# Mixing weights of a dilated-attention kernel: statistics loaded by GpSimd's queue, small operations moved to GpSimd and spread over steps, additions later, chunks closer

## The chip, the core and the metric

The kernel runs on one core of a Trainium2 chip. The metric is the device time of one execution in microseconds (us); the median of several runs counts.

## What is computed

One layer of a decoder trunk over 2048 tokens and 1024 channels, in float32. Half of the channels go through eight attention heads of 64, the other half through pooling groups; both are projected by `w_out`; then come a gated MLP and a gated per-layer embedding. The change is in the attention. Each head attends in three patterns, and the outputs are mixed by their softmax denominators:

```python
DIL_PATTERNS = ((128, 1), (512, 4), (2048, 16))
...
for window, dil in DIL_PATTERNS:
    o, m, d = _dilated_branch(q, k, v, slopes, window, dil)   # output, row max, denominator
...
w = d * jnp.exp(m - jnp.max(m, axis=0, keepdims=True))
w = w / jnp.sum(w, axis=0, keepdims=True)
return jnp.sum(w[..., None] * o, axis=0)
```

## The kernel before

It runs in three phases: projection, attention, and the rest (output projection, MLP, gate). Matrix products are made from split operands: a rounded high part and the remainder as a low part. The attention phase lies at about 389 to 655 us.

**The steps of the attention.** The kernel merges the two wider patterns into one, called far; the narrow one is near. So each query has two outputs, near and far, and two pairs of statistics (`st1` near, `st3` far: row extremum, with the sign turned so that it is a minimum, and denominator). The work is cut into 128 steps s: 8 heads by 16 blocks of 128 queries. A pair of heads takes 32 steps. One step holds far and near scores on TensorE (L568 to L580), a reduction for each on VectorE (L584 near, L590 far), an exponential for each on ScalarE (L596, L600), transposes on TensorE (L610), the high part on ScalarE (L623) and the low part on VectorE (L627), and the products with the values on TensorE (L638 far, L652 near). Stages of one query block stand in different steps; the list `CFG["ord"]` gives each stage's place in a step and its lag. On TensorE, VectorE, ScalarE and GpSimd the program's order is kept as written. The order of the transfers that SyncE issues is made by the scheduling layer.

**Copying out.** Every four steps a group of queries is done. `copy_out` (L670 on) copies the output from PSUM to a buffer `ev` (far by ScalarE, near by VectorE, L676), has SyncE move one half of it across partitions into `s1` or `s3` (L677), and puts an addition of the other half on GpSimd (L678) three steps later.

**Mixing.** When the first, second and third pair of heads has ended, its two outputs are mixed while the next pair runs. d counts the steps from the pair's end (`mix`, L727 on):

- at the end `mix_stats` (L788) transposes the statistics on TensorE and copies them to SBUF on VectorE; at d = 1 ScalarE's queue stores them to DRAM (L803, L804);
- at d = 4 ScalarE's queue loads them back in another layout (L811 `sn`, L815 `sf`), each load 512 pieces of 64 bytes;
- at d = 9 `mix_lift` (L885): on VectorE the minimum `lo` (L889) and two differences `ex` (L892, L893), on ScalarE the exponential `wts` (L894);
- at d = 10 `mix_weights` (L897): on VectorE two products and a sum, the denominator `dn` (L901 to L903), its reciprocal `rs` (L905) and the weights (L906); GpSimd's queue stores them (L907);
- for each of four chunks c of 512 queries, `mix_fetch` (L912) at d = 13 + 7c has SyncE load the weights broadcast over partitions, and `mix_steps` (L940) six steps later begins two products and a sum on GpSimd (L946, L948, L955) and a store of the mixed chunk (L958). After the third pair, which is called quick, the fetches are at d = 12 + 4c, and two parts are issued a step.

The fourth pair is mixed at the end of the phase by other code. `last_weights` (L847) makes its weights on VectorE and ScalarE, and its scratch `lo` shares the buffers `m1` with the chunks.

Of the kernel before, what the change touches and what calls it, by code (L numbers as in the profile page):

```python
# [10 lines left out]
F32 = mybir.dt.float32  # L11
F32R = mybir.dt.float32r
AF = mybir.ActivationFunctionType
ALU = mybir.AluOpType
# [3 lines left out]
P = 128  # L18
# [8 lines left out]
CH = 512  # L27
# [16 lines left out]
CFG = {"tt": 2, "ee": 2, 'ord': [['B', 0], ['G', 0], ['M', 0], ['h', 2], ['N', 0], ['F', 0], ['nm', 0], ['p', 7], ['o', 8], ['ne', 0], ['V', 6], ['fm', 0], ['l', 2], ['W', 6], ['S', 1], ['fe', 0], ['T', 1]], 'perm': [3, 1, 2, 0], 'fp': [[0], [1], [2], [3]], 'np': [[0, -1], [1], [2], [3]], 'm': [9, 10, 13, 4, 6, 7]}  # L44
# [6 lines left out]
def fp(ap):  # L51
    return ap.bitcast(F32)
# [439 lines left out]
def phase_attention(tc, g, mx, near_b, far_b):  # L492
# [3 lines left out]
    nc = tc.nc  # L496
    NS = H * NQ
    LAST = 4 * H - 2
    with ExitStack() as ctx:
        sb = ctx.enter_context(tc.tile_pool(name="b_sb", bufs=1, reuse_waits="tile"))  # L500
# [5 lines left out]
        heads, steps, groups, pairs = {}, {}, {}, {}  # L506
# [155 lines left out]
        sums = Ticker()  # L662

        def halves(pt, gi, near):
            h, q = divmod(gi, 4)
            e = h % 2
            mine = slice(DH * e, DH * e + DH)
            other = slice(DH * (1 - e), DH * (1 - e) + DH)
            return e, mine, other, pt.s1[:, q * CH : (q + 1) * CH] if near else pt.s3[:, q, :]

        def copy_out(copy, gi, near):

            e, mine, other, dst = halves(pairs[gi // 8], gi, near)
            o = groups[gi].o[near]
            t = sb.tile([P, CH], F32, tag="ev", bufs=8, name="ev")
            copy(t, o)  # L676
            nc.sync.dma_start(dst[mine], t[other])  # L677
            sums.later(3, lambda: nc.gpsimd.tensor_tensor(dst[mine], dst[mine], t[mine], op=ALU.add))  # L678

        def add_out(gi, near):  # L680
            e, mine, other, dst = halves(pairs[gi // 8], gi, near)
# [25 lines left out]
        def fold(v):  # L707
            gi, part = v // 4, v % 4
            if part == 1 and gi < LAST:
                copy_out(nc.scalar.copy, gi, False)  # L710

        def folded(v):
            gi, part = v // 4, v % 4
            if part % 2 and gi >= LAST:
                add_out(gi, part == 3)
            elif part == 3:
                copy_out(nc.vector.tensor_copy, gi, True)
            if part == 3:
                groups.pop(gi)
# [7 lines left out]
        def mix(s):  # L727
            for pr in range(NPAIR - 1):
                d = s - (pr + 1) * 2 * NQ
                if d == 1:  # L730
                    mix_stats_store(nc, g, pr, pairs[pr])
                if d == 4:
                    mix_stats_load(nc, g, mx, pr, pairs[pr])
                if d == CFG["m"][0]:
                    mix_lift(nc, g, mx, pairs[pr])
                if d == CFG["m"][1]:
                    mix_weights(nc, g, mx, pr, pairs[pr])
                for c in range(NCH):
                    quick = pr == NPAIR - 2
                    at = d - (12 + 4 * c if quick else 13 + 7 * c)  # L740
                    if at == 0:
                        mix_fetch(nc, g, mx, nc.sync, pr, pairs[pr], c)
                    if at == 6:
                        ops[pr, c] = mix_steps(nc, g, mx, pr, pairs[pr], c)
                    for _ in range(1 + quick if (pr, c) in ops else 0):
                        next(ops[pr, c], None)
# [6 lines left out]
        with tc.manual_schedule(engines=set(EN.values())):  # L753
            for dst, src in load_qk(0):
                rdma(nc, dst, src)
            for q in range(4):
# [3 lines left out]
            stages = {  # L760
                "F": far_scores, "N": near_scores, "fm": far_max, "nm": near_max, "fe": far_exp, "ne": near_exp,
                "T": turn, "h": high, "l": low, "V": values, "W": values_b, "S": stats, "M": mix, "o": fold, "p": folded, "B": begin, "G": shifts
            }
            for s in range(NS + 10):
# [37 lines left out]
def mix_stats_store(nc, g, pr, pt):  # L802
    nc.scalar.dma_start(g.std[pr], pt.sx)  # L803
    nc.scalar.dma_start(g.stf[pr], pt.sy)  # L804


def mix_stats_load(nc, g, sb, pr, pt):
    q = nc.scalar
    pt.sn = sb.tile([P, 2, 2, 16], F32, tag="sn", name="sn")
    pt.sf = sb.tile([P, 2, 2, 16], F32, tag="sf", name="sf")  # L810
    q.dma_start(  # L811
        pt.sn.rearrange("p a e r -> p (a e) r"),
        g.std[pr].rearrange("(ae n) q -> ae (n q)", n=NQ).rearrange("ae (i r) -> i ae r", r=16),
    )
    q.dma_start(  # L815
        pt.sf.rearrange("p a e r -> p (a e) r"),
        g.stf[pr].rearrange("(ae n) q -> ae (n q)", n=4).rearrange("ae (i r) -> i ae r", r=16),
    )
# [28 lines left out]
def last_weights(nc, sb, pt):  # L847

    both = (pt.near, pt.far)
    lo = sb.tile([P, CH], F32, tag="m1", bufs=2, name="lo")[:8]  # L850
    nc.vector.tensor_tensor(lo, pt.near[0], pt.far[0], op=ALU.min)
    yield
    for mx_, _ in both:
        nc.vector.tensor_tensor(mx_, lo, mx_, op=ALU.subtract)
    yield
    for ex, _ in both:
        nc.scalar.activation(ex, ex, AF.Exp)
    yield
    for ex, dn in both:
        nc.vector.tensor_tensor(dn, ex, dn, op=ALU.mult)  # L860
    yield
    nc.vector.tensor_tensor(lo, pt.near[1], pt.far[1], op=ALU.add)
    yield
    nc.vector.reciprocal(lo, lo)
    yield
    pt.w = []
    for ex, _ in both:
        hi, low = (sb.tile([P, CH], F32R, tag=f"wb{y}", bufs=2, name=f"w{y}")[:8] for y in range(2))
        nc.vector.tensor_tensor(ex, ex, lo, op=ALU.mult)
        nc.scalar.copy(hi, ex)  # L870
        nc.vector.tensor_tensor(low, ex, fp(hi), op=ALU.subtract)
        pt.w.append((hi, low))
    yield
# [11 lines left out]
def mix_lift(nc, g, sb, pt):  # L885

    sn, st3 = pt.sn, pt.sf
    lo = sb.tile([P, 2, 16], F32, tag="lo", name="lo")
    nc.vector.tensor_tensor(lo, sn[:, 0], st3[:, 0], op=ALU.min)  # L889
    pt.wts = sb.tile([P, 2, 2, 16], F32, tag="wts", name="wts")  # L890
    ex = sb.tile([P, 2, 2, 16], F32, tag="ex", name="ex")
    nc.vector.tensor_tensor(ex[:, 0], lo, sn[:, 0], op=ALU.subtract)  # L892
    nc.vector.tensor_tensor(ex[:, 1], lo, st3[:, 0], op=ALU.subtract)  # L893
    nc.scalar.activation(pt.wts, ex, AF.Exp)  # L894


def mix_weights(nc, g, sb, pr, pt):  # L897

    sn, st3, wts = pt.sn, pt.sf, pt.wts
    dn = sb.tile([P, 2, 2, 16], F32, tag="dn", name="dn")  # L900
    nc.vector.tensor_tensor(dn[:, 0], wts[:, 0], sn[:, 1], op=ALU.mult)  # L901
    nc.vector.tensor_tensor(dn[:, 1], wts[:, 1], st3[:, 1], op=ALU.mult)
    nc.vector.tensor_tensor(dn[:, 0], dn[:, 0], dn[:, 1], op=ALU.add)  # L903
    rs = sb.tile([P, 2, 16], F32, tag="rs", name="rs")
    nc.vector.reciprocal(rs, dn[:, 0])  # L905
    nc.vector.tensor_tensor(wts, wts, rs[:, None, :, :].to_broadcast([P, 2, 2, 16]), op=ALU.mult)  # L906
    nc.gpsimd.dma_start(  # L907
        g.wd[pr].rearrange("ae (i r) -> i ae r", r=16), wts.rearrange("p a e r -> p (a e) r")
    )


def mix_fetch(nc, g, sb, q, pr, pt, c, bufs=2):  # L912

    cs = slice(c * CH, (c + 1) * CH)
    wb = []
    for a in range(2):
        w = sb.tile([P, CH], F32, tag=f"wb{a}", bufs=bufs, name=f"wb{a}")
        for e in range(2):
            q.dma_start(w[e * DH : e * DH + DH], g.wd[pr][2 * a + e, None, cs].to_broadcast([DH, CH]))
        wb.append(w)  # L920
    pt.__dict__.setdefault("wb", {})[c] = wb
# [18 lines left out]
def mix_steps(nc, g, sb, pr, pt, c):  # L940

    cs = slice(c * CH, (c + 1) * CH)
    wb = pt.wb.pop(c)
    m1 = sb.tile([P, CH], F32, tag="m1", bufs=2, name="m1")
    m3 = sb.tile([P, CH], F32, tag="m3", bufs=1, name="m3")
    nc.gpsimd.tensor_tensor(m1, pt.s1[:, cs], wb[0], op=ALU.mult)  # L946
    yield
    nc.gpsimd.tensor_tensor(  # L948
        m3.rearrange("p (i r) -> p i r", r=4),
        pt.s3.rearrange("p r i -> p i r")[:, c * P : c * P + P, :],  # L950
        wb[1].rearrange("p (i r) -> p i r", r=4),
        op=ALU.mult,
    )
    yield
    nc.gpsimd.tensor_tensor(m1, m1, m3, op=ALU.add)  # L955
    yield
    yield
    nc.gpsimd.dma_start(g.mr[pr][:, cs], m1)  # L958
    yield
# [1103 lines left out]
```

## Time and profile before

| | us |
|---|---|
| median of 3 runs | 2370.11 (2368.89 to 2372.66) |
| profiled execution | 2374.07 |
| its span | 2372.3 |
| TensorE (PE) busy | 2312.0 (97%) |
| VectorE (DVE) busy | 1701.3 (72%) |
| ScalarE (ACT) busy | 1124.9 (47%) |
| GpSimd (POOL) busy | 566.0 (24%) |
| attention, 389 to 652: PE / DVE / ACT / POOL busy | 242.1 / 224.5 / 226.2 / 130.0 of 263 |

The span runs from the first to the last instruction; the execution's time has a little around it. The shares are averages over phases with different limits: in the attention phase three engines are nearly full at once, so that a stop of any one of them soon stops the others. PEld is TensorE's weight load, and ACTq, SPq, POOLq are the issues of transfers on an engine's queue. A wait is shown as the instruction that waited and the one that came last by the profile.

### The profile page before, as it was taken

Reading aid. Unit: us, or ns where it says so; the run is one execution under the profiler, and the core shown is the slowest. Engines: PE = TensorE matmul, PEld = TensorE weight load, DVE = VectorE, ACT = ScalarE, POOL = GpSimd, SP = SyncE. Lnnn points to the kernel's source line nnn. Section 1 sums busy time; section 2 is a strip of 40 time slices with the busy share of each in tenths; the row PEclk is TensorE's granted clock in tenths of the full one; section 3 lists DMA queues with packets and bytes.
Section 4 is the critical chain, followed back from the end, with each engine's and each line's share of the span. In section 5 each row is a group of like instructions: output and inputs, shape, how many; then the busy total and the mean of one; then the engine's idle time right before and its main releaser. Section 6 shows DMA issues by size and latency. Waiting matters only on the chain.

```text
span 2372.3 us, 32820 instructions
## 1 busy us (share of the span) xinstructions
PE 2312.0 (97%) x11279; PEld 1957.9 (83%) x11279; DVE 1701.3 (72%) x2681; ACT 1124.9 (47%) x2044; POOL 566.0 (24%) x544
## 2 busy tenths in 40 slices
PE   8999999999889999999999999999999999999998
PEld 7988888898868878888887888888788888888888
DVE  6735436888864678999999999777765656655664
ACT  5423325888822245454446444444554444444331
POOL 1412221356610133343430666000010000001000
PEclk9999999999999999999999999999999999999999
DMA  7635446787576664556567878544497776754332
GB/s 255 214 120 191 151 164 236 235 255 251 145 256 213 213 217 142 194 184 204 191 226 234 272 265 283 164 131 147 152 344 235 243 241 196 235 165 147 119 103 94
DMA packets 240553, 476.02 MB, mean 201 GB/s; under 512 B 37472, under 2 KB 63904, under 8 KB 237312
## 3 DMA queue, kind: packets, MB, share of 16 engines
q1 hardware_dynamic: 205040, 394.64, 50.6%
q0 software_dynamic: 15696, 51.49, 6.2%
q10 hardware_dynamic: 19648, 27.77, 3.3%
q8 instruction: 89, 1.46, 0.3%
q14 instruction: 80, 0.66, 0.1%
HBM read 309.14 MB, written 156.79 MB: 196 GB/s over the span
## 4 chain that ended last, share of the span: by engine, by line
PE 85%; DVE 5%; DMA 5%; issue 2%; ACT 1%; POOL 0%; ACTq 0%; SPq 0%; DVEq 0%; POOLq 0%
PE ua L1396 19%; PE uc L1396 9%; PE dn L89 5%; PE dn L90 5%; PE dn L91 5%; PE z L89 5%; PE z L90 5%; PE ub L1396 5%; PE z L91 5%; PE o L91 2%; PE o L89 2%; PE o L90 2%; PE gp L89 2%; PE gp L91 2%; PE gp L90 2%
## 5 line engine op out<-in xcount | busy, mean ns | idle before, releaser
L90 PE MATMUL dn<-al,wu 128*128 128x512 f32 x616 | 240.1, 390 | 2.2 <-DVE al L85 2.2
L89 PE MATMUL dn<-ah,wu 128*128 128x512 f32 x616 | 240.2, 390 | 0.0
L91 PE MATMUL dn<-ah,wu 128*128 128x512 f32 x616 | 239.8, 389 | 0.0
L85 DVE TENSOR_TENSOR al<-ra,ah 128x512 fp32r<-128x512 f32 x154 | 105.8, 689 | 108.4 <-ACT ah L84 108.2
L89 PE MATMUL z<-hnh,wh 128*128 128x512 f32 (+1 forms) x480 | 168.8, 352 | 7.8 <-ACT hnh L258 6.0
L90 PE MATMUL z<-hnl,wh 128*128 128x512 f32 (+1 forms) x480 | 168.3, 351 | 0.1
L91 PE MATMUL z<-hnh,wl 128*128 128x512 f32 (+1 forms) x480 | 167.9, 350 | 0.0
L84 ACT CAST ah<-ra 128x512 fp32r<-128x512 f32 x154 | 95.2, 621 | 142.6 <-PE dn L91 132.0
L90 PEld LDWEIGHTS dn<-al,wu 128*128 128x128 f32 x616 | 115.6, 188 | 27.1 <-DVE al L85 3.3
L89 PEld LDWEIGHTS dn<-ah,wu 128*128 128x128 f32 x616 | 115.6, 188 | 24.6 <-ACT ah L84 0.8
L91 PEld LDWEIGHTS dn<-ah,wu 128*128 128x128 f32 x616 | 115.6, 188 | 24.2
L85 DVE TENSOR_TENSOR wu<-ru,wu 128x1024 fp32r<-128x1024 f32 x88 | 132.3, 1504 | 0.0
L1396 PE MATMUL uc<-s3h,wu 128*128 128x512 f32 x352 | 116.4, 391 | 1.3 <-ACT s3h L1452 1.3
L1396 PE MATMUL ua<-s4h,wu 128*128 128x512 f32 x352 | 117.3, 394 | 0.0
L1396 PE MATMUL ua<-s2h,wu 128*128 128x512 f32 x352 | 115.8, 390 | 1.4 <-ACT ug L1598 1.2
L1396 PE MATMUL ua<-s1h,wu 128*128 128x512 f32 x352 | 115.6, 389 | 0.9 <-ACT ug L1624 0.9
L85 DVE TENSOR_TENSOR wu<-rw,wu 128x512 fp32r<-128x512 f32 x149 | 100.9, 686 | 21.6 <-ACT wu L84 21.5
L1396 PE MATMUL uc<-a22h,wu 128*128 128x512 f32 x352 | 115.6, 389 | 0.0
L1396 PE MATMUL ub<-a12h,wu 128*128 128x512 f32 x352 | 115.6, 389 | 0.0
L1396 PE MATMUL ua<-a11h,wu 128*128 128x512 f32 x352 | 115.6, 389 | 0.0
L89 PEld LDWEIGHTS z<-hnh,wh 128*128 128x128 f32 x480 | 92.8, 193 | 19.8 <-ACT hnh L258 6.0
L155 DVE TENSOR_TENSOR acc<-acc,sq 128x512 f32<-128x512 f32 (+1 forms) x118 | 79.1, 671 | 41.8 <-ACT sq L154 30.7
(337 smaller groups left out, 6644.5 us busy)
## 6 DMA issues: line engine op xcount, KB each, us to landing
ru<-in_w_up_dram SPq DMA_DIRECT2D x66, 512.0 KB, 4.3
wr<-in_w_in_dram SPq DMA_DIRECT2D x64, 256.0 KB, 4.8
rw<-in_w_down_dram SPq DMA_DIRECT2D x61, 256.0 KB, 4.1
nt<-h SPq DMA_DIRECT2D x56, 256.0 KB, 3.8
td<-t SPq DMA_DIRECT2D x22, 512.0 KB, 2.6
t<-td SPq DMA_DIRECT2D x22, 512.0 KB, 3.8
nt<-in_w_down_dram POOLq DMA_DIRECT2D x44, 256.0 KB, 5.4
ra<-oq0s SPq DMA_DIRECT2D x44, 256.0 KB, 3.6
```

What stands on the lines that cost most here:

```text
L84: nc.scalar.copy(hi, src)
L85: (low or nc.gpsimd).tensor_tensor(lo, src, fp(hi), op=ALU.subtract)
L89: nc.tensor.matmul(ps, wh, ah, start=first, stop=False, skip_group_check=again)
L90: nc.tensor.matmul(ps, wh, al, start=False, stop=False, skip_group_check=again)
L91: nc.tensor.matmul(ps, wl, ah, start=False, stop=last, skip_group_check=again)
L155: nc.vector.tensor_tensor(acc[:, :n], acc[:, :n], sq[:, :n], op=ALU.add)
L1396: nc.tensor.matmul(pst, x[:, ksl], y, start=first and k == 0 and n == 0, stop=k == HK - 1 and n == 2, skip_group_check=True)
```

## The change

Six edits, all around the mixing of the first three pairs:

- the load of the statistics moves from ScalarE's queue at d = 4 to GpSimd's queue at d = 3;
- of the small operations VectorE keeps the minimum (d = 9) and the reciprocal; the differences, the products, the sum and the scaling of the weights go to GpSimd;
- the steps are spread: differences at d = 9, exponential and denominator at d = 13, reciprocal, weights and their store at d = 16;
- the additions of copied results are put five steps later in place of three;
- the chunks are fetched at d = 18 + 5c (third pair 18 + 2c), and their products begin six (third pair three) steps later;
- the scratch of the fourth pair's weights has a buffer `lo8` of its own.

```diff
-            sums.later(3, lambda: nc.gpsimd.tensor_tensor(dst[mine], dst[mine], t[mine], op=ALU.add))
+            sums.later(5, lambda: nc.gpsimd.tensor_tensor(dst[mine], dst[mine], t[mine], op=ALU.add))
...
-                if d == 4:
+                if d == 3:
                     mix_stats_load(nc, g, mx, pr, pairs[pr])
-                if d == CFG["m"][0]:
+                if d == 9:
                     mix_lift(nc, g, mx, pairs[pr])
-                if d == CFG["m"][1]:
+                if d == 13:
+                    nc.scalar.activation(pairs[pr].wts, pairs[pr].ex, AF.Exp)
+                if d == 16:
+                    mix_shares(nc, g, mx, pr, pairs[pr])
+                if d == 13:
                     mix_weights(nc, g, mx, pr, pairs[pr])
                 for c in range(NCH):
                     quick = pr == NPAIR - 2
-                    at = d - (12 + 4 * c if quick else 13 + 7 * c)
+                    at = d - (18 + 2 * c if quick else 18 + 5 * c)
                     if at == 0:
                         mix_fetch(nc, g, mx, nc.sync, pr, pairs[pr], c)
-                    if at == 6:
+                    if at == (3 if quick else 6):
...
 def mix_stats_load(nc, g, sb, pr, pt):
-    q = nc.scalar
+    q = nc.gpsimd
...
 def last_weights(nc, sb, pt):
-    lo = sb.tile([P, CH], F32, tag="m1", bufs=2, name="lo")[:8]
+    lo = sb.tile([P, CH], F32, tag="lo8", name="lo8")[:8]
...
 def mix_lift(nc, g, sb, pt):
...
-    nc.vector.tensor_tensor(ex[:, 0], lo, sn[:, 0], op=ALU.subtract)
-    nc.vector.tensor_tensor(ex[:, 1], lo, st3[:, 0], op=ALU.subtract)
-    nc.scalar.activation(pt.wts, ex, AF.Exp)
+    nc.gpsimd.tensor_tensor(ex[:, 0], lo, sn[:, 0], op=ALU.subtract)
+    nc.gpsimd.tensor_tensor(ex[:, 1], lo, st3[:, 0], op=ALU.subtract)
...
 def mix_weights(nc, g, sb, pr, pt):
...
-    nc.vector.tensor_tensor(dn[:, 0], wts[:, 0], sn[:, 1], op=ALU.mult)
-    nc.vector.tensor_tensor(dn[:, 1], wts[:, 1], st3[:, 1], op=ALU.mult)
-    nc.vector.tensor_tensor(dn[:, 0], dn[:, 0], dn[:, 1], op=ALU.add)
+    nc.gpsimd.tensor_tensor(dn[:, 0], wts[:, 0], sn[:, 1], op=ALU.mult)
+    nc.gpsimd.tensor_tensor(dn[:, 1], wts[:, 1], st3[:, 1], op=ALU.mult)
+    nc.gpsimd.tensor_tensor(dn[:, 0], dn[:, 0], dn[:, 1], op=ALU.add)
+    pt.dn = dn
+
+
+def mix_shares(nc, g, sb, pr, pt):
...
-    nc.vector.reciprocal(rs, dn[:, 0])
-    nc.vector.tensor_tensor(wts, wts, rs[:, None, :, :].to_broadcast([P, 2, 2, 16]), op=ALU.mult)
+    nc.vector.reciprocal(rs, pt.dn[:, 0])
+    nc.gpsimd.tensor_tensor(wts, wts, rs[:, None, :, :].to_broadcast([P, 2, 2, 16]), op=ALU.mult)
```

What this does to the queues is seen in the program's order. On VectorE after the first pair, before the change, the minimum and all that hangs on it stand within two steps (ISA tt is the reduction of a step's scores, ptl the low part of a step):

```order
L889 TENSOR_TENSOR lo<-sn,sf 128x32
L892 TENSOR_TENSOR ex<-lo,sn 128x32
L893 TENSOR_TENSOR ex<-lo,sf 128x32
L584 ISA tt,st_4803<-sn,nb_4400 128x256
L584 ISA st_4803 128x1
L590 ISA tt,st_4804<-sf,fb_4401 128x256
L590 ISA st_4804 128x1
L627 TENSOR_TENSOR ptl<-tp,pth 128x384
L901 TENSOR_TENSOR dn<-wts,sn 128x32
L902 TENSOR_TENSOR dn<-wts,sf 128x32
L903 TENSOR_TENSOR dn<-dn 128x32
L905 RECIPROCAL rs<-dn 128x32
```

After the change the minimum stands at the same place (line numbers are four to nine higher in the changed kernel):

```order
L627 TENSOR_TENSOR ptl<-tp,pth 128x640
L893 TENSOR_TENSOR lo<-sn,sf 128x32
L584 ISA tt,st_4803<-sn,nb_4399 128x256
L584 ISA st_4803 128x1
L590 ISA tt,st_4804<-sf,fb_4400 128x256
```

Seven steps on, VectorE has the reciprocal alone between two steps:

```order
L590 ISA tt,st_4804<-sf,fb_4400 128x128
L590 ISA st_4804 128x1
L627 TENSOR_TENSOR ptl<-tp,pth 128x512
L914 RECIPROCAL rs<-dn 128x32
L584 ISA tt,st_4803<-sn,nb_4844 128x256
L584 ISA st_4803 128x1
```

So six of the eight small operations (the scaling L906, next in the first list, among them) have left VectorE, and the minimum has kept its place.

On GpSimd after the second pair, before the change, only the weights' store stands between additions and the first pair's last chunk (names with their numbers; m1 and m3 are the chunk's products, wb0 and wb1 the broadcast weights):

```order
L946 TENSOR_TENSOR m1_5987<-s1_4003,wb0_5813 128x512
L678 TENSOR_TENSOR s1_4805<-s1_4805,ev_5943 64x512
L948 TENSOR_TENSOR m3_5988<-s3_4004,wb1_5816 128x512
L955 TENSOR_TENSOR m1_5987<-m1_5987,m3_5988 128x512
L907 DMA wd1_124<-wts_6017 128x4x16
L678 TENSOR_TENSOR s3_5733<-s3_5733,ev_6029 64x512
L958 DMA mr0_95<-m1_5987 128x512
```

After the change the differences stand right behind the products of that last chunk, and the denominators behind two additions that wait for copies:

```order
L955 TENSOR_TENSOR m1_5963<-s1_4003,wb0_5776 128x512
L957 TENSOR_TENSOR m3_5964<-s3_4004,wb1_5779 128x512
L964 TENSOR_TENSOR m1_5963<-m1_5963,m3_5964 128x512
L896 TENSOR_TENSOR ex_6017<-lo_6014,sn_5848 128x32
L897 TENSOR_TENSOR ex_6017<-lo_6014,sf_5849 128x32
L678 TENSOR_TENSOR s3_4806<-s3_4806,ev_5909 64x512
L678 TENSOR_TENSOR s1_4805<-s1_4805,ev_5942 64x512
L967 DMA mr0_95<-m1_5963 128x512
L904 TENSOR_TENSOR dn_6128<-wts_6016,sn_5848 128x32
L905 TENSOR_TENSOR dn_6128<-wts_6016,sf_5849 128x32
L906 TENSOR_TENSOR dn_6128<-dn_6128 128x32
```

The two loads stand further ahead in the same queue, before the sum of the chunk before. What was a chain of VectorE and ScalarE is now one that goes to and fro between GpSimd and the two. TensorE's order is the same.

## Prediction before the run

> **What bounds the kernel now.** I read the engines' busy shares first, then the windows of the attention stage (389 to 655 us), the starts of its steps, the waits in it, and the transfers. The head of the page:
>
> ```profile
> span 2372.3 us, 32820 instructions
> PE 2312.0 (97%) x11279; PEld 1957.9 (83%) x11279; DVE 1701.3 (72%) x2681; ACT 1124.9 (47%) x2044; POOL 566.0 (24%) x544
> ```
>
> TensorE bounds the whole, so a gain can only lie where TensorE goes idle. Two windows of the attention stage (columns: length; busy us of PE, PEld, DVE, ACT, POOL with counts; granted clock; DMA share; GB/s):
>
> ```profile
> 485.00:518.00 33.00, 32.05 (x226) 30.86 (x226) 28.05 (x92) 29.14 (x88) 19.08 (x16) 1.00 0.86 254
> 518.00:552.00 34.00, 28.36 (x172) 26.47 (x173) 28.06 (x83) 24.93 (x76) 20.44 (x18) 0.85 0.79 241
> ```
>
> The first is quiet: TensorE is busy 97% of it, VectorE and ScalarE are close behind. In the second, just after a pair of heads ends, TensorE stands for 5.6 us and its clock dips to 0.85. How long the steps take is read from the near-scores reduction L584, one per step. First 16 quiet steps, then the first 16 steps after the first, second and third pair (17 starts bound 16 steps):
>
> ```profile
> L584 DVE CUSTOM_DVE_ANT_0 tt<-sn,nb x17: 277/424/426, 483.2 to 512.2; 128x256 f32<-128x256 f32 x16, 128x128 f32<-128x128 f32 x1
> L584 DVE CUSTOM_DVE_ANT_0 tt<-sn,nb x17: 280/415/426, 448.3 to 483.2; 128x256 f32<-128x256 f32 x16, 128x128 f32<-128x128 f32 x1
> L584 DVE CUSTOM_DVE_ANT_0 tt<-sn,nb x17: 281/415/425, 512.2 to 552.7; 128x256 f32<-128x256 f32 x16, 128x128 f32<-128x128 f32 x1
> L584 DVE CUSTOM_DVE_ANT_0 tt<-sn,nb x17: 279/415/426, 581.8 to 620.7; 128x256 f32<-128x256 f32 x16, 128x128 f32<-128x128 f32 x1
> ```
>
> Quiet: 29.0 us (1.81 a step). After the pairs: 34.9, 40.5 and 38.9, so 5.9, 11.5 and 9.9 too long, 27.3 together. The first four of these steps (d = 0 to 3) make and store the statistics, which the change leaves alone; quiet ones first again:
>
> ```profile
> L584 DVE CUSTOM_DVE_ANT_0 tt<-sn,nb x5: 277/424/425, 483.2 to 490.5; 128x256 f32<-128x256 f32 x4, 128x128 f32<-128x128 f32 x1
> L584 DVE CUSTOM_DVE_ANT_0 tt<-sn,nb x5: 280/414/425, 448.3 to 457.6; 128x256 f32<-128x256 f32 x4, 128x128 f32<-128x128 f32 x1
> L584 DVE CUSTOM_DVE_ANT_0 tt<-sn,nb x5: 281/415/425, 512.2 to 522.1; 128x256 f32<-128x256 f32 x4, 128x128 f32<-128x128 f32 x1
> L584 DVE CUSTOM_DVE_ANT_0 tt<-sn,nb x5: 279/415/425, 581.8 to 591.0; 128x256 f32<-128x256 f32 x4, 128x128 f32<-128x128 f32 x1
> ```
>
> 7.3 quiet against 9.3, 9.9 and 9.2: 2.0, 2.6 and 1.9 stay. What the change touches is the rest: 3.9, 8.9 and 8.0, together **20.8 us**. It is the most that the edits on the statistics can return.
>
> **The change part by part.** What fills the 20.8 us, from the waits of the stage (engine and line, what was waited for: total us, times, longest):
>
> ```profile
> ACT pth L623 <- PE sf L569: 4.3, 2, 2.3
> ACT pth L623 <- PE sn L580: 1.5, 1, 1.5
> DVE lo L889 <- DMA sf<-stf: 3.2, 2, 2.4
> ```
>
> *The load leaves ScalarE's queue.* The first two rows are put down to TensorE, which had long been done. ScalarE stands there at d = 4 behind its own load, which waits until the stored statistics have landed: 2.3, 1.5 and 2.0 us in the three pairs. That ends. The wait now stands on GpSimd at d = 3; queued behind it there are copied results to add and a chunk's products, which nobody needs for many steps.
>
> *The small operations.* Grouped by line, then VectorE's minimum, the first of them, in each pair in order of time (start, length; in brackets the idle time before):
>
> ```profile
> L889 DVE TENSOR_TENSOR lo<-sn,sf 128x32 f32<-128x32 f32 x3 | 2.6, 862 | 3.2 <-DMA sf<-stf 3.2
> L892 DVE TENSOR_TENSOR ex<-lo,sn 128x32 f32<-128x32 f32 x3 | 2.8, 932 | 0.1
> L893 DVE TENSOR_TENSOR ex<-lo,sf 128x32 f32<-128x32 f32 x3 | 0.5, 181 | 0.0
> L905 DVE RECIPROCAL rs<-dn 128x32 f32<-128x32 f32 x3 | 1.1, 353 | 0.1
> 468.50 1.22 DVE L889 TENSOR_TENSOR lo<-sn,sf 128x32 f32<-128x32 f32 x1
> 534.73 0.77 DVE L889 TENSOR_TENSOR lo<-sn,sf 128x32 f32<-128x32 f32 x1 [2.36 <-DMA sf<-stf]
> 602.56 0.60 DVE L889 TENSOR_TENSOR lo<-sn,sf 128x32 f32<-128x32 f32 x1 [0.87 <-DMA sf<-stf]
> ```
>
> Operations of one size take 181 ns (L893) or, on the mean, 932 (L892). I read the long ones as held up by a GpSimd operation under way, which takes about as long (1.28 us, row below). Two stay on VectorE, the minimum and the reciprocal. I charge them in full: 862 + 353 ns, 1.2 us a pair, **3.6 us** in all. Bounds: 0.18 + 0.35 a pair (the minimum as short as its like), 1.6 in all; or a minimum of 0.18 held up by one whole GpSimd product of 1.28 us (its row follows), which with the reciprocal makes 1.8 a pair and 5.4. The difference 20.8 - 3.6 = **17.2 us** is returned if the statistics are there in time.
>
> The moved ones lengthen GpSimd's work. The same product on both engines, and a small copy on GpSimd as the lower bound of a small operation:
>
> ```profile
> L946 POOL TENSOR_TENSOR m<-s,wb x12: 1262/1283/1295, 486.9 to 650.9; 128x512 f32<-128x512 f32 x12
> L929 DVE TENSOR_TENSOR m<-s,wb x4: 680/682/689, 675.3 to 688.6; 128x512 f32<-128x512 f32 x4
> L425 POOL COPY u<-tail x16: 191/197/719, 111.7 to 363.8; 128x15 f32<-128x15 f32 x16
> ```
>
> Six operations of 0.2 us (up to 1.28, a full-size one) are 1.2 to 7.7 us a pair on an engine that is busy 19.08 of 33 us in the quiet window, and the new places leave four steps from the differences to the exponential, three (5.4 us) from the denominators to the reciprocal. I take nothing for them; without that cover each late us would cost ScalarE one at the exponential or VectorE one at the reciprocal. The Trainium skill (GPSIMD Engine Reference, section 3.1) speaks against such a move: elementwise work belongs on VectorE, where it is about twice as fast. The 1283 against 682 ns above agree; by that rule the sum would lose some 2 us more a pair if GpSimd stood on the path, and by the slack it loses none.
>
> *Does the load land in time?* Its source is ready when ScalarE could issue it before; then come the landing times of that load, of a small store and of two chunk stores on GpSimd's queue, these two in the same busy stretches after the second and third pair:
>
> ```profile
> 458.72 0.43 ACTq L811 DMA_DIRECT2D sn<-std  x1
> 522.03 0.37 ACTq L811 DMA_DIRECT2D sn<-std  x1
> 523.37 0.37 ACTq L815 DMA_DIRECT2D sf<-stf  x1
> 592.11 0.40 ACTq L811 DMA_DIRECT2D sn<-std  x1
> DMA to landing us min/median/max: 5.4/9.9/11.3
> L907 POOL DMA_DIRECT2D wd<-wts x3: 787/798/807, 473.2 to 609.2; - x3
> mr<-m POOLq DMA_DIRECT2D x1, 256.0 KB, 7.1
> mr<-m POOLq DMA_DIRECT2D x1, 256.0 KB, 6.4
> ```
>
> Without ScalarE's stop VectorE reaches the minimum at 468.5 - 2.3 = 466.2, 534.7 - 2.4 - 1.5 = 530.8 and 602.6 - 0.9 - 2.0 = 599.7. GpSimd issues the second load 0.8 us after the first (the 798 ns of a store in as many pieces), so at 459.5, 523.4 (its source was late) and 592.9. On ScalarE's queue's 9.9 or 11.3 us it would come too late in two pairs; on the chunk stores' 6.4 to 7.1 it lands at 465.9 to 466.6, 530.5 and 599.3, about when it is wanted. Which queue's time holds is told by the packets, between 440 and 490 us, where ScalarE's queue carried four transfers of 32 KB and GpSimd's one:
>
> ```profile
> q10 hardware_dynamic: 1168, 0.13, 1.9%
> q0 software_dynamic: 32, 0.03, 0.2%
> ```
>
> The same 512 pieces of 64 bytes go as hundreds of packets from ScalarE and as 32 from GpSimd. If the busy DMA engines take turns by packet, GpSimd's load waits for few turns. I take it as in time, no wait.
> The Trainium skill (DMA: Bandwidth & Descriptors, section "Issuing engine by pattern") says the opposite of the order: ScalarE's and SyncE's queues are generally the faster. By the landings of ScalarE's queue the sum would be the late case below, 9.6 us in place of 17.2. No run here shows a load of this form on GpSimd's queue.
>
> *Additions two steps later, chunks closer.* These order GpSimd's and SyncE's queues alone; the adds get 3.6 us more for their transfers, whose waits cost only GpSimd. At the end of the stage:
>
> ```profile
> 655.06 1.81 DVE L851 TENSOR_TENSOR lo<-nr,fr 8x512 f32<-8x512 f32 x1
> 658.63 0.67 DVE L854 TENSOR_TENSOR fr<-lo,fr 8x512 f32<-8x512 f32 x1
> 655.04 1.28 POOL L678 TENSOR_TENSOR s<-s,ev 64x512 f32<-64x512 f32 x1
> 656.87 1.28 POOL L678 TENSOR_TENSOR s<-s,ev 64x512 f32<-64x512 f32 x1
> ```
>
> Beside these two additions VectorE's operation takes 1.81 in place of 0.67 us. The minimum of the last weights now has a buffer of its own, but it had not waited for one. The four chunks of the third pair start three steps later and in half the spacing, with the same operations before the end; four additions stand last. Either they are over before (gain 2 x 1.14 = 2.3 us) or one more is in the way (loss 1.2); I take 0.
>
> **Sum.** 20.8 - 3.6 + 0 = 17.2 us. The profiled execution took 2374.07 us, its span of 2372.3 and 1.8 around it, and becomes 2356.9; it lies 0.17% over the median of the three runs shown. That median, 2370.11, becomes **2352.9**. Bounds in this case: gain 20.8 - 5.4 - 1.2 = 14.2 to 20.8 - 1.6 + 2.3 = 21.5, so 2348.6 to 2355.9.
>
> **The rivals.** *The load lands late* (0.25). GpSimd's queue has no better place among the transfers. Then the minimum starts as late as before plus the slower issue, 0.4 us: in the second pair 1.5 + 2.4 + 0.4 + 1.2 of the 8.9 stay, in the third 2.0 + 0.9 + 0.4 + 1.2 of the 8.0, in the first (5.4 us) only 1.2 of 3.9. Gain 3.4 + 3.5 + 2.7 = 9.6, so 2360.5. For it: the stretch is full of the next heads' loads, whoever issues. The Trainium skill (DMA: Bandwidth & Descriptors, section "SWDGE vs HWDGE vs iDMA") has each engine take turns between queues, switching at packets, which would rather speak for the early landing.
>
> *Nothing returned* (0.07). If those loads set the pace of the steps, the engines would wait for them wherever the statistics are made, and the time stays at 2370. Against it: ScalarE's and VectorE's stops alone account for the lost steps.
>
> *GpSimd becomes a funnel* (0.06), the case on the other side. It is one queue in order, now between statistics and reciprocal. If an addition ahead of the denominators waits for its copy as long as the longest such landing, 13.1 us, VectorE stands at the reciprocal with all behind it:
>
> ```profile
> DMA to landing us min/median/max: 2.2/3.5/13.1
> ```
>
> With three steps (5.4 us) of slack that is 7.7 us a pair, 23.1 in all, less 17.2: 5.9 slower, 2376.0. It decides from a hold of 5.4 + 17.2 / 3 = 11.1 us in every pair. Against it: the median is 3.5 and the adds now have five steps (9.1 us).
>
> **How the numbers follow.** The forecast has 0.62. A measurement can tell about 0.2% (4.7 us) from no change. Faster: forecast and late load, 0.87; same: 0.07; slower: the funnel, 0.06. The range takes the forecast's bounds and the late case with a margin of about 1.5 us for the scatter of runs (2368.89 to 2372.66): 2347.5 to 2362.0.
>
> **What would show it.** Right: no idle of ScalarE at d = 4; the minimum without a wait for its load; 16 steps after a pair in 31 to 36 us; the load landing within 7 us. Late case: the minimum waits 2 to 4 us in the second and third pair. Wrong altogether: the reciprocal waits for GpSimd, or steps after the pairs as long as now.

## The result, and the profile after

| | before | changed |
|---|---|---|
| median of 6 runs (us) | 2371.74 (2368.89 to 2373.55) | 2353.38 (2348.91 to 2358.88) |
| profiled execution | 2374.07 | 2356.13 |

The ratio is 0.9925 (95%: 0.9910 to 0.9940), 18.4 us less. The forecast was 17.2 us less. The changed kernel's page begins:

```profile
span 2354.1 us, 32813 instructions
PE 2307.5 (98%) x11279; PEld 1955.0 (83%) x11279; DVE 1697.9 (72%) x2663; ACT 1125.0 (48%) x2044; POOL 571.9 (24%) x568
```

The work is the same, the span 18.2 us shorter. The window of the attention stage just after the second pair's end (same columns as before):

```profile
513.00:547.00 34.00, 33.46 (x235) 32.31 (x234) 31.08 (x98) 32.74 (x100) 24.47 (x26) 1.00 0.96 305
```

TensorE, idle for 5.6 of 34 us there before, now is for 0.5, and its clock does not dip. GpSimd's share rises to 24.5 of 34, and hardly anybody stands for it. The starts of the steps, first over 16 steps after each pair, then over d = 0 to 3:

```profile
L584 DVE CUSTOM_DVE_ANT_0 tt<-sn,nb x17: 280/417/425, 446.9 to 477.8; 128x256 f32<-128x256 f32 x16, 128x128 f32<-128x128 f32 x1
L584 DVE CUSTOM_DVE_ANT_0 tt<-sn,nb x17: 280/415/426, 506.9 to 538.9; 128x256 f32<-128x256 f32 x16, 128x128 f32<-128x128 f32 x1
L584 DVE CUSTOM_DVE_ANT_0 tt<-sn,nb x17: 280/415/426, 567.6 to 601.7; 128x256 f32<-128x256 f32 x16, 128x128 f32<-128x128 f32 x1
L584 DVE CUSTOM_DVE_ANT_0 tt<-sn,nb x5: 280/411/424, 446.9 to 456.2; 128x256 f32<-128x256 f32 x4, 128x128 f32<-128x128 f32 x1
L584 DVE CUSTOM_DVE_ANT_0 tt<-sn,nb x5: 280/414/425, 506.9 to 516.3; 128x256 f32<-128x256 f32 x4, 128x128 f32<-128x128 f32 x1
L584 DVE CUSTOM_DVE_ANT_0 tt<-sn,nb x5: 280/414/425, 567.6 to 576.9; 128x256 f32<-128x256 f32 x4, 128x128 f32<-128x128 f32 x1
```

The 16 steps take 30.9, 32.0 and 34.1 us in place of 34.9, 40.5 and 38.9: 17.3 us less, nearly all of the 18.2. The first four still take 9.3, 9.4 and 9.2 (7.3 when quiet; starts taken to hundredths from here on). The other twelve, quiet 21.7, are too long by 0, 0.9 and 3.2, together 4.0 us in place of 20.8.

The groups of the changed lines in the attention stage (busy us, mean ns, idle before):

```profile
L893 DVE TENSOR_TENSOR lo<-sn,sf 128x32 f32<-128x32 f32 x3 | 2.4, 814 | 1.3 <-DMA sf<-stf 1.3
L914 DVE RECIPROCAL rs<-dn 128x32 f32<-128x32 f32 x3 | 1.0, 347 | 0.2 <-POOL dn L906 0.2
L915 POOL TENSOR_TENSOR wts<-wts,rs 128x64 f32<-128x64 f32 x3 | 1.0, 323 | 1.9 <-DVE rs L914 1.8
L896 POOL TENSOR_TENSOR ex<-lo,sn 128x32 f32<-128x32 f32 x3 | 0.8, 252 | 3.1 <-DVE lo L893 3.1
L737 ACT ACTIVATE wts<-ex 128x64 f32<-128x64 f32 x3 | 0.7, 241 | 0.0
```

The minimum waits once for its load, the reciprocal once for 0.2 us, the exponential never. A small operation takes 0.25 to 0.32 us on GpSimd. The landing times of the two loads, `sn` and then `sf`:

```profile
DMA to landing us min/median/max: 3.0/4.9/5.6
DMA to landing us min/median/max: 4.3/5.2/7.1
```

### The profile page after: what moved, and what is told of

It is laid out like the page before. It is cut to its first block, busy times and chain, and to the rows that moved or that the text cites. A ratio compares the mean times of both kernels' runs of the same rounds, so it can differ in the third digit from the quotient of the medians.

```text
span 2354.1 us, 32813 instructions
## 1 busy us (share of the span) xinstructions
PE 2307.5 (98%) x11279; PEld 1955.0 (83%) x11279; DVE 1697.9 (72%) x2663; ACT 1125.0 (48%) x2044; POOL 571.9 (24%) x568
## 4 chain that ended last, share of the span: by engine, by line
PE 86%; DVE 5%; DMA 4%; issue 2%; ACT 2%; POOL 1%; SPq 0%; DVEq 0%; POOLq 0%; ACTq 0%
PE ua L1405 18%; PE uc L1405 9%; PE dn L90 5%; PE dn L89 5%; PE dn L91 5%; PE z L89 5%; PE z L90 5%; PE z L91 5%; PE ub L1405 5%; PE o L91 2%; PE o L89 2%; PE o L90 2%; PE tp L610 2%; PE gp L89 2%; PE gp L90 2%
```

## What had filled the time before

The prediction left out one view of the kernel before, ScalarE's timeline over the steps d = 4 to 15. These are all its stops of 1 us and more there, in brackets with what ended them:

```profile
460.00 0.69 ACT L623 CAST pth<-tp 128x640 fp32r<-128x640 f32 x1 [2.31 <-PE sf L569]
470.08 0.26 ACT L894 ACTIVATE wts<-ex 128x64 f32<-128x64 f32 x1 [1.38 <-DVE ex L893]
523.78 0.69 ACT L623 CAST pth<-tp 128x640 fp32r<-128x640 f32 x1 [1.53 <-PE sn L580]
536.97 0.26 ACT L894 ACTIVATE wts<-ex 128x64 f32<-128x64 f32 x1 [4.48 <-DVE ex L893]
541.65 0.51 ACT L596 ACTIVATE ee<-tt,st 128x256 f32<-128x256 f32 x1 [1.89 <-DVE st L584]
593.10 0.69 ACT L623 CAST pth<-tp 128x640 fp32r<-128x640 f32 x1 [1.99 <-PE sf L569]
604.64 0.26 ACT L894 ACTIVATE wts<-ex 128x64 f32<-128x64 f32 x1 [2.84 <-DVE ex L893]
609.33 0.51 ACT L596 ACTIVATE ee<-tt,st 128x256 f32<-128x256 f32 x1 [1.90 <-DVE st L584]
```

They add to 3.7, 7.9 and 6.7 us, 18.3 in all, against the 3.9, 8.9 and 8.0 (20.8) that the steps lost. The load's stop is 5.8 of it. The largest, 8.7, is the exponential: it stands in the step of the minimum, so ScalarE waits until VectorE has waited for the load and done minimum and differences. Then 3.8: a step later VectorE does denominators and weights ahead of the next scores. In the changed kernel the same view shows, of stops over 0.6 us:

```profile
527.07 0.51 ACT L596 ACTIVATE ee<-tt,st 128x256 f32<-128x256 f32 x1 [0.62 <-DVE st L584]
588.80 0.51 ACT L596 ACTIVATE ee<-tt,st 128x256 f32<-128x256 f32 x1 [1.80 <-DVE st L584]
```

Both stand behind VectorE's minimum, which was long in these pairs.

## The experiments

The theory: load, minimum's wait and VectorE's small operations fill the 20.8 us, and the load (with its late landing) is worth 8 to 9. The rival: what counts is the distance in steps between an operation and the engine that waits for it, whoever does it. "Lost" is by how much the steps d = 4 to 15 after the three pairs exceed the quiet 21.7 us in that kernel's own trace, of which there is one for each row. Ratios are to the kernel before, run beside each, and compare the means of the runs.

| kernel | median (us) | ratio (95%) | lost after the pairs (us) |
|---|---|---|---|
| before | 2371.74 | 1 | 3.9 + 8.9 + 8.0 |
| changed | 2353.38 | 0.9925 (0.9910 to 0.9940) | 0.0 + 0.9 + 3.2 |
| changed, again | 2351.93 | 0.9923 (0.9911 to 0.9935) | 0.7 + 0.3 + 0.5 |
| load alone | 2367.22 | 0.9976 (0.9966 to 0.9985) | 2.3 + 7.0 + 5.6 |
| order alone | 2369.69 | 0.9983 (0.9974 to 0.9992) | 3.3 + 6.7 + 7.5 |
| load undone | 2358.38 | 0.9941 (0.9928 to 0.9955) | 1.7 + 2.1 + 3.4 |
| operations back | 2357.64 | 0.9932 (0.9919 to 0.9944) | 0.5 + 3.4 + 3.1 |
| both undone: spread and order | 2360.08 | 0.9950 (0.9934 to 0.9965) | 3.9 + 2.2 + 2.3 |
| spread and order, again | 2359.69 | 0.9947 (0.9936 to 0.9958) | 1.6 + 2.1 + 2.4 |
| not spread | 2367.59 | 0.9985 (0.9975 to 0.9995) | 1.5 + 7.6 + 2.6 |
| minimum two steps later | 2360.85 | 0.9956 (0.9942 to 0.9970) | 0.0 + 5.9 + 2.6 |
| load late | 2367.49 | 0.9983 (0.9974 to 0.9991) | 0.7 + 9.8 + 9.1 |
| statistics a step later | 2356.83 | 0.9932 (0.9920 to 0.9944) | 0.0 + 0.0 + 0.0 |

**One part alone.** In the kernel before, the load goes to GpSimd's queue:

```diff
-                if d == 4:
+                if d == 3:
                     mix_stats_load(nc, g, mx, pr, pairs[pr])
...
-    q = nc.scalar
+    q = nc.gpsimd
```

> The kernel before, with one edit: the statistics are loaded by GpSimd's queue at d = 3. My theory: ScalarE's stop behind its own load goes (5.8 us in three pairs before) and the load lands in 5 to 7 us, so that VectorE's minimum no longer waits for it (3.2 us before); the small operations on VectorE keep their cost. That makes 8 to 9 us less than the kernel before, about 2363, and the 16 steps after the three pairs take about 33, 36.5 and 35.5 us. Rival, the landing is the same on either queue: the wait moves from ScalarE to the minimum, 2 to 4 us in the second and third pair, and no more than 3 us are gained. Rival, the order of additions and chunks makes the gain: 0.

It gained 5.7 us (3.6 to 8.1), less than the 8 to 9 expected and about the load's own stop of 5.8. Most of the largest stop stayed, in its waits:

```profile
ACT wts L894 <- DVE ex L893: 6.3, 3, 3.0
DVE lo L889 <- DMA sf<-stf: 1.2, 2, 0.7
```

The minimum hardly waited now, yet the exponential still stood for 6.3 us: that stop is not the load's alone. Next, in the kernel before, only the additions, the chunks and the scratch are changed:

```diff
-            sums.later(3, lambda: nc.gpsimd.tensor_tensor(dst[mine], dst[mine], t[mine], op=ALU.add))
+            sums.later(5, lambda: nc.gpsimd.tensor_tensor(dst[mine], dst[mine], t[mine], op=ALU.add))
...
-                    at = d - (12 + 4 * c if quick else 13 + 7 * c)
+                    at = d - (18 + 2 * c if quick else 18 + 5 * c)
...
-                    if at == 6:
+                    if at == (3 if quick else 6):
...
-    lo = sb.tile([P, CH], F32, tag="m1", bufs=2, name="lo")[:8]
+    lo = sb.tile([P, CH], F32, tag="lo8", name="lo8")[:8]
```

> The kernel before with only the other edits: additions five steps later, chunks at the new steps, the scratch lo8 with a buffer of its own; load and small operations as before. My theory: no change beyond 2 us either way, 2370 to 2373, and the 16 steps after the pairs as long as before. Rival, a less crowded queue of transfers is what helped: 5 us or more are gained.

It gained 4.0 us (1.9 to 6.2), more than the nothing predicted. ScalarE still stood for 7.7 us at the exponential and for 6.4 at d = 4; but its two stops of 1.9 us behind VectorE's denominators and weights are gone. The sum of the denominators after the second and third pair, before and then here:

```profile
538.42 1.43 DVE L903 TENSOR_TENSOR dn<-dn 128x32 f32<-128x32 f32 x1
606.08 1.43 DVE L903 TENSOR_TENSOR dn<-dn 128x32 f32<-128x32 f32 x1
```

```profile
538.67 0.19 DVE L903 TENSOR_TENSOR dn<-dn 128x32 f32<-128x32 f32 x1
605.18 0.19 DVE L903 TENSOR_TENSOR dn<-dn 128x32 f32<-128x32 f32 x1
```

Before, a product of the last chunk ran on GpSimd beside it (L948, at 538.22 for 1.56 us and at 605.89 for 1.58); with the chunks and additions moved, GpSimd is idle there. VectorE's eight small operations took 6.7 us in place of 13.3. In this trace the gain thus comes from GpSimd's long operations no longer standing beside them; additions and chunks were not varied apart. Its minimum waited longer for its load than before, 4.6 us in the third pair.

**One part undone.** In the changed kernel, the load back on ScalarE at d = 4; then, in another, the six operations back on VectorE in their new steps:

```diff
-                if d == 3:
+                if d == 4:
                     mix_stats_load(nc, g, mx, pr, pairs[pr])
...
-    q = nc.gpsimd
+    q = nc.scalar
```

```diff
-    nc.gpsimd.tensor_tensor(ex[:, 0], lo, sn[:, 0], op=ALU.subtract)
+    nc.vector.tensor_tensor(ex[:, 0], lo, sn[:, 0], op=ALU.subtract)
...
-    nc.gpsimd.tensor_tensor(dn[:, 0], wts[:, 0], sn[:, 1], op=ALU.mult)
+    nc.vector.tensor_tensor(dn[:, 0], wts[:, 0], sn[:, 1], op=ALU.mult)
...
-    nc.gpsimd.tensor_tensor(wts, wts, rs[:, None, :, :].to_broadcast([P, 2, 2, 16]), op=ALU.mult)
+    nc.vector.tensor_tensor(wts, wts, rs[:, None, :, :].to_broadcast([P, 2, 2, 16]), op=ALU.mult)
```

> The changed kernel with the load put back on ScalarE's queue at d = 4, all else as changed. My theory: the stop of ScalarE (some 5 us) and the wait of the minimum (3 us or more) come back, the small operations stay cheap: 8 to 9 us of the gain of 17 are lost, about 2362. The load lands in 8 to 11 us in the second and third pair, in hundreds of packets. Rival, the queue does not matter once the steps are spread: the time stays at 2353.

> The changed kernel with all small operations on VectorE again, at their new spread steps (differences at d = 9, denominators at d = 13, reciprocal and scaling at d = 16). My theory: what counts is VectorE's time, lengthened where GpSimd computes; up to 8 us of the gain are lost, the time is 2357 to 2361. Rival, it is the spreading that gained, since a short operation in a step hides in its slack: no more than 2 us are lost, 2353 to 2355.

With the load undone less was lost than the theory asked: 3.8 us by the ratios (0.9941 against 0.9925), not 8 to 9, and the intervals overlap. The stops of ScalarE at d = 4 are back, but not the minimum's wait (its waits, then the landings of `sn` and `sf`):

```profile
ACT pth L623 <- PE sf L569: 4.3, 2, 2.2
DVE lo L893 <- DMA sf<-stf: 0.5, 1, 0.5
```

```profile
DMA to landing us min/median/max: 3.5/4.6/6.2
DMA to landing us min/median/max: 5.1/5.9/9.4
```

With a third such stop of 2.5 us, which the profile puts down to another matrix product, the stops make 6.7 of the 7.1 us that its steps lose. The load by ScalarE does not land as late as in the kernel before, where it took up to 11.3 us: the sum "on ScalarE's queue it comes too late" does not hold in this kernel. (With the order alone it still took up to 13.5.) With the operations back on VectorE the median, 2357.64, lies in the theory's range, but by the ratios beside the kernel before (0.9932 against 0.9925, 1.7 us) the time cannot be told from the changed kernel's. In its trace five of VectorE's small operations, beside GpSimd's, took 1.0 to 1.4 us, ScalarE stood behind them for up to 1.8 us, and the steps lost 6.9 us. The Trainium skill (GPSIMD Engine Reference, section 3.1: elementwise work is about twice as fast on VectorE) speaks for this version; the rows have the small ones closer (0.25 us on GpSimd, 0.18 on VectorE when nothing holds it up), and the time does not tell the two kernels apart.

**The spread without the moves, and the moves without the spread.** The two edits just shown, made together, leave the new steps, additions and chunks. The other way round, load and operations stay moved, and the steps go back:

```diff
-                if d == 13:
+                if d == 9:
                     nc.scalar.activation(pairs[pr].wts, pairs[pr].ex, AF.Exp)
-                if d == 16:
-                    mix_shares(nc, g, mx, pr, pairs[pr])
-                if d == 13:
+                if d == 10:
                     mix_weights(nc, g, mx, pr, pairs[pr])
+                    mix_shares(nc, g, mx, pr, pairs[pr])
```

> The changed kernel with the load on ScalarE's queue at d = 4 and all small operations on VectorE: of the change only the spread steps and the order of additions and chunks remain. After the first four runs I hold that the spreading itself carries much of the gain, since before the change ScalarE stood at the exponential until VectorE's differences were done, and VectorE needed the exponential one step later. Theory: 8 to 12 us less than the kernel before, 2361 to 2365. Rival, each engine's share counts by itself: without load and moved operations nothing is left but the order, 2368 to 2370.

> The changed kernel, load and small operations on GpSimd, but the exponential again at d = 9 and denominators, reciprocal and scaling at d = 10; chunks and additions as changed. Theory: ScalarE stands at the exponential for GpSimd's differences and VectorE at the reciprocal for GpSimd's denominators; most of the gain is lost or more: 2364 to 2376, with a wait of ScalarE at the exponential of 2 to 5 us a pair. Rival, the engine that does the small operations is what counts: 2353 to 2356.

> The kernel with only spread steps and order (load on ScalarE's queue, small operations on VectorE) once more, beside the changed kernel. If load and engine together are worth 4 us or more on top of the spreading, it stays above the changed kernel by that: 0.994 to 0.9965 of the kernel before. If they are worth nothing, it is level with it.

> The changed kernel once more, unaltered, beside the three others of this set. Expected 0.9925 of the kernel before, within 0.9905 to 0.9945.

The spread counts both ways. With the spread and the order, but load and operations where they were, the ratio is 0.9950 and 0.9947: 12 us, 8 more than the order alone. The exponential, still fed by VectorE, stands for nothing (its group in the first of the two), while VectorE's small operations take 6.7 us as with the order alone, so it is not shorter operations that were gained:

```profile
L737 ACT ACTIVATE wts<-ex 128x64 f32<-128x64 f32 x3 | 0.7, 241 | 0.0
```

With all but the spread the ratio is 0.9985, no better than the order alone. The waits show what is lost, though the minimum never waited for its load there:

```profile
ACT wts L737 <- POOL ex L896: 8.5, 3, 6.3
DVE rs L913 <- POOL dn L905: 3.0, 3, 1.0
```

The exponential's stop is as large as before; it is now GpSimd that comes late. The two stops make 11.5 of the 11.7 us that the steps lose. Yet 11.7 is 9.1 less than before, as much as the load and the order return in their own traces (5.9 and 3.3), while the time shows only 3.6. This trace reached the attention at 394.6 us, the others at 389.1 to 391.2, ahead of every edit; whether all runs of this kernel start late is not known. So the spread is worth some 8 us by the times without the moves and 14 with them, by the steps 9 to 12 and 8 to 10. Of the 9 to 12 some 3.5 are a later landing of the load in the trace of the order alone.

On top of the spread, load and engine do count: beside each other on one chip, 0.9947 (0.9936 to 0.9958) without them and 0.9923 (0.9911 to 0.9935) with them, 7.8 us by the medians and 5.7 by the means. Their shares are not told apart.

**The distance to the exponential.** In the changed kernel the minimum and differences go to d = 11, so that no load is late:

```diff
-                if d == 9:
+                if d == 11:
                     mix_lift(nc, g, mx, pairs[pr])
```

> The changed kernel with the minimum and differences two steps later, at d = 11. Theory: in the third pair the minimum no longer waits for its load (1.3 us) and the steps after the third pair lose 1 to 2 us; the exponential at d = 13 still finds its differences done. 2351 to 2353. Rival, the two steps are then too few for GpSimd and ScalarE stops at the exponential: 2354 to 2358.

The theory lost, and by more than the rival's 1 to 5 us: some 7 by the ratios. The load's wait went, but two steps are too few for GpSimd: after the second pair it reaches the differences 7 us after the minimum, behind two additions that waited 4.2 and 1.0 us for their copies. The exponential's wait:

```profile
ACT wts L737 <- POOL ex L897: 6.9, 2, 4.2
```

**The queues at the same moment.** The changed kernel loads the same data once more by ScalarE's queue at d = 5, into two tiles that nobody reads:

```diff
+                if d == 5:
+                    mix_stats_again(nc, g, mx, pr, pairs[pr])
...
+def mix_stats_again(nc, g, sb, pr, pt):
...
+    nc.scalar.dma_start(
+        ta.rearrange("p a e r -> p (a e) r"),
+        g.std[pr].rearrange("(ae n) q -> ae (n q)", n=NQ).rearrange("ae (i r) -> i ae r", r=16),
+    )
...
```

> The changed kernel plus a second load of the same statistics by ScalarE's queue at d = 5 into tiles that nobody reads, about when GpSimd's queue loads them. The time is read no further than that it stays near the changed kernel's. Theory of the prediction: turns by packet let GpSimd's loads land first, in 4 to 7 us against 8 to 11 us in the second and third pair, with 16 to 32 packets a load against 512. Rival, the queue makes no difference at equal moments: both land within 1 us of each other, and the landing depends on when they are issued.

After the second pair the four loads were issued between 516.3 and 517.2 us. Their landings there, then the packets in the stretch after the first pair (440 to 480 us):

```profile
sn<-std POOLq DMA_DIRECT2D x1, 32.0 KB, 5.3
ta<-std ACTq DMA_DIRECT2D x1, 32.0 KB, 7.7
sf<-stf POOLq DMA_DIRECT2D x1, 32.0 KB, 7.1
tb<-stf ACTq DMA_DIRECT2D x1, 32.0 KB, 12.4
```

```profile
q10 hardware_dynamic: 1168, 0.13, 2.3%
q0 software_dynamic: 64, 0.07, 1.0%
```

After the third pair it is 4.4 and 6.9 against 7.8 and 12.4, after the first 6.5 and 6.2 against 7.1 and 7.2. So in full stretches GpSimd's queue does land first, with 64 packets for its two loads. The Trainium skill (DMA: Bandwidth & Descriptors, section "Issuing engine by pattern") calls ScalarE's queue generally the faster; in this form and this traffic it is not. That the packets are the reason fits, but was not varied by itself; the kernel was run once.

**A late load.** The load goes to ScalarE at d = 6, where nothing makes ScalarE wait:

```diff
-                if d == 3:
+                if d == 6:
...
-    q = nc.gpsimd
+    q = nc.scalar
```

> The changed kernel with the load on ScalarE's queue at d = 6, when the stored statistics have landed and ScalarE does not stop. Theory (the queue sets the landing): 7 to 12 us from d = 6 in the second and third pair, the minimum three steps (5.4 us) later waits 2 to 6 us in each, and the time is 2358 to 2364. Rival, the landing is no longer on this queue: 2353 to 2356.

It lost some 15 us of the gain (0.9983 against 0.9923), more than either side expected. Two loads landed after 13.6 and 13.8 us, and the minimum (start, length, idle before) stood for them:

```profile
534.18 0.19 DVE L893 TENSOR_TENSOR lo<-sn,sf 128x32 f32<-128x32 f32 x1 [7.97 <-DMA sf<-stf]
603.73 0.19 DVE L893 TENSOR_TENSOR lo<-sn,sf 128x32 f32<-128x32 f32 x1 [7.75 <-DMA sf<-stf]
```

The lost 9.8 and 9.1 of these pairs are these waits and 1 to 2 us to get going again. Here each us by which the minimum comes late is a lost one.

**All a step later.** The statistics' making, store, load and every later step move by one (lag of stage `S` 2, store at d = 2, load 4, differences 10, exponential and denominator 14, weights 17, chunks from 19):

```diff
-... ['S', 1], ...
+... ['S', 2], ...
...
-                if d == 1:
+                if d == 2:
                     mix_stats_store(nc, g, pr, pairs[pr])
...
```

> The changed kernel with the statistics made one step later and all that follows them too. Of the 6.3 us that the first four steps after the three pairs lose in the changed kernel as before, part is TensorE's and VectorE's mutual wait for the transposed statistics (2.8 and 2.7 us). Theory: one step later these are ready, 2 to 4 us less than the changed kernel, 2349 to 2352. Rival, the transposes and copies cost the same wherever they stand: 2353.

No step from d = 4 on was disturbed: 21.7 us for twelve after each pair. The first four take 9.1 instead of 9.3, so their loss is in making the statistics, not in where this stands. The first and last step of the attention in this kernel's trace, and in the changed kernel's second one:

```profile
L584 DVE CUSTOM_DVE_ANT_0 tt<-sn,nb x128: 277/421/426, 390.1 to 625.8; 128x256 f32<-128x256 f32 x120, 128x128 f32<-128x128 f32 x8
```

```profile
L584 DVE CUSTOM_DVE_ANT_0 tt<-sn,nb x128: 280/416/427, 389.7 to 627.0; 128x256 f32<-128x256 f32 x120, 128x128 f32<-128x128 f32 x8
```

In this trace the stage is 1.6 us shorter than in the changed kernel's second one, but the median, 2356.83, does not beat 2351.93. Nothing here is shown to be faster than the changed kernel. The changed kernel's six runs beside it lie at 2351.3 to 2352.0 four times and at 2357.5 and 2357.8. What makes the 6 us is open; behind the start of the attention's last step, where little was edited, the kept traces already differ by as much (1720.8 to 1726.6 us).

## Why the prediction was right, and where not

- *What the steps lose* (20.8 us after d = 3): right, and the bound held. Of it 16.8 came back by the traces; 17.2 was forecast. The other 1.4 between the spans is 0.5 in the first four steps and 1.5 by which this execution reached the attention earlier, which the change does not touch, less 0.6 in the rest. The first and last steps of before, then of the changed kernel:

```profile
L584 DVE CUSTOM_DVE_ANT_0 tt<-sn,nb x128: 277/416/426, 391.2 to 648.3; 128x256 f32<-128x256 f32 x120, 128x128 f32<-128x128 f32 x8
```

```profile
L584 DVE CUSTOM_DVE_ANT_0 tt<-sn,nb x128: 277/416/426, 389.7 to 629.3; 128x256 f32<-128x256 f32 x120, 128x128 f32<-128x128 f32 x8
```

- *What fills the 20.8* is the step that failed. The prediction put it on the load's stop (5.8), the minimum's wait (3.2) and, for the rest, VectorE's small operations. The spread it counted only as cover for the slower GpSimd. But that wait is part of the 8.7 for which ScalarE stood at the exponential, a row of the waits that the prediction did not quote. With load and operations moved but not spread, that stop was still 8.5 and 11.7 of the 20.8 stayed lost; with the spread and neither moved, 12 us of time came back. The total came out right because the sum took the whole loss as gone, whatever filled it: as to the cause that is luck. "Small operations" and "spread" should have been two terms, the second of some 8 us or more.
- *Minimum and reciprocal stay: 3.6.* The residue is 4.0, but not as the 1.2 a pair that was charged. The reciprocal cost nothing that shows. The minimum took 0.18 us in the first pair, 1.23 and 1.03 in the others and waited 1.3 once; its third pair alone makes 3.2 of the 4.0. The changed kernel's second trace lost only 1.6 in all, so this term is no better known than that.
- *The load lands in 6.4 to 7.1:* it took 3.0 to 7.1, and the two queues at the same moment bear it out. Its counterpart, ScalarE's queue being too late by its 9.9 to 11.3, did not hold at d = 4 once the steps were spread (5.1 to 9.9 for `sf`) and did at d = 6 (13.6 and 13.8). The late case was priced at 7.6 us less gain; the load at d = 6 cost 15.
- *GpSimd as a funnel:* not in the changed kernel (0.2 us at the reciprocal). With fewer steps of slack it is there: 6.9 us at the exponential with two, 8.5 with none.
- *End of the stage, 0:* the fourth pair's minimum and differences still stand beside GpSimd's last four additions:

```profile
636.05 1.15 DVE L855 TENSOR_TENSOR lo<-nr,fr 8x512 f32<-8x512 f32 x1
637.23 1.64 DVE L858 TENSOR_TENSOR nr<-lo,nr 8x512 f32<-8x512 f32 x1
638.79 1.74 DVE L858 TENSOR_TENSOR fr<-lo,fr 8x512 f32<-8x512 f32 x1
```

  Together they take 4.5 us; before it was 4.3. Neither gain nor loss.
- *Additions and chunks:* taken at nothing, as ordering two queues alone; by themselves they gave 4.0 us (1.9 to 6.2). The prediction had read VectorE's long operations as held up by GpSimd's, but not that this edit moves GpSimd's long ones away from them.

In the steps the parts roughly add: load and order return 5.9 and 3.3, both with the operations moved but not spread 9.1, and the spread the next 8 to 10. So moving the operations without more steps returned nothing of its own. In the times they do not add: 5.7 and 4.0 alone, 3.6 together. The late start of that one trace would account for most of the difference, but one trace does not show that.

## What to carry to other kernels

Where several engines are nearly full and hand work to each other in one step, list the stops of every one of them, and add these up until they make the lost time, before putting prices on operations. A round trip between engines is hidden by the number of steps between its parts; who does the small operations came second here, and moving them to an engine with a queue without adding steps only moved the wait. Look also at what runs beside them: moving GpSimd's long operations away shortened VectorE's. A load whose landing decides should be issued as early as its source allows, on a queue on which it does not hold an engine.

## What the runs showed of the hardware

- VectorE's minimum was held up until GpSimd operations under way were over. In the changed kernel, first VectorE's three, then GpSimd's two that the long ones ran beside:

```profile
465.29 0.18 DVE L893 TENSOR_TENSOR lo<-sn,sf 128x32 f32<-128x32 f32 x1
525.40 1.23 DVE L893 TENSOR_TENSOR lo<-sn,sf 128x32 f32<-128x32 f32 x1
587.34 1.03 DVE L893 TENSOR_TENSOR lo<-sn,sf 128x32 f32<-128x32 f32 x1 [1.30 <-DMA sf<-stf]
```

```profile
525.31 1.28 POOL L955 TENSOR_TENSOR m<-s,wb 128x512 f32<-128x512 f32 x1
586.81 1.50 POOL L957 TENSOR_TENSOR m<-s,wb 128x512 f32<-128x512 f32 x1
```

  The minimum ends at 526.63 and 588.37, the others at 526.59 and 588.31; with GpSimd idle it takes 0.18 us. The Trainium skill (SBUF — State Buffer, section "Who interferes with whom") states that a VectorE operation with two inputs in SBUF contends with a GpSimd instruction that reads SBUF; the trace agrees.
- One kernel's traces differ by 2.4 us in the same twelve steps (4.0 and 1.6 lost), and its runs by 6 us in one set and 10 in the other, so that parts worth less are told only by repeated runs.
